# Router one chunk behind the output projection, shared experts beside the lists, and the last expert blocks in one accumulator

## The chip, the cores and the metric

The kernel runs on one core of a Trainium2 chip. The metric is device time in microseconds (us) of one execution, the median of several. The core's engines run instruction streams of their own: PE (TensorE, matrix products and transposes), DVE (VectorE), ACT (ScalarE), POOL (GpSimd) and SP (SyncE, which here only issues DMA transfers). The granted clock of PE is a number from 0 to 1 beside each stretch of a profile.

## The reference

One block of a diffusion model on 512 tokens of width 1024: a token mixer (retention and gated DeltaNet over the whole grid of tokens, merged by gates), its output projection, and a mixture of experts. The change touches what comes behind the mixer's merge. Cut to that:

```python
x  = x + g1 * _rmsnorm(merged @ w_o, norm_mix_post)          # 512 x 1024
h2 = _rmsnorm(x, norm_ffn_pre) * (1.0 + sc2) + sh2
x  = x + g2 * _rmsnorm(_moe(h2), norm_ffn_post)
...
def _moe(h):                       # 64 experts of width 256, 8 for each token
    scores = sigmoid(h @ w_router) # biased; top 4 of 8 groups, then top 8 experts
    wts = scores of the 8 chosen / their sum * 2.5
    routed[token] += wts * ((silu(xe @ w_gate[e]) * (xe @ w_up[e])) @ w_down[e])
    shared = (silu(h @ w_sh_gate) * (h @ w_sh_up)) @ w_sh_down
    return routed + shared
```

## The kernel before

The kernel is written in stages for a framework that schedules instructions: each engine keeps one program order, tiles from rotating pools make an instruction wait until the buffer's last reader is done, and semaphores are put in by the framework. The written order sets the order on each engine only roughly (a scheduler moves instructions between neighbours), so the engine orders shown under the change are those of the built programs.

**phaseO** is the output projection with all that depends on it. The projection's weights come as two column halves (c = 0, 1) of 512, and each half runs over four chunks t of 128 tokens. A projection of a chunk and half is 24 matmuls (eight k steps of three, since each operand is split in a high and a low part; L111 to L113). In the second half, each chunk goes through everything before the next starts: the square and scaling of the projection (L1086, L1087), the normalisation and residual (L1093 to L1097, which give x1 and store it to `out`), the pre-normalised row `h2` (L1099 to L1103, stored to `h2d` for the gathers), eight transposes of it (L1110) copied into `h2T` (L1111), the router `router(t)` (16 matmuls L1010, a sigmoid L1012, 26 small instructions on DVE L1013 to L1039 that give `sel` and the weights `wt`), and the shared expert `shared(t)` (64 matmuls L1054, Silu L1057, product L1058, eight wide matmuls L1063, copies L1064, store of y to the accumulator `accd[0]` in DRAM, L1065). `accd[1]` is filled with zeros (L1117).

**phaseM** starts the loads of the first experts' weights (L1156, buffers of 1 MB each: four `w`, two `wgu` that share memory with earlier tiles, three `wd`), and then makes the list of tokens for each expert: `left` is loaded (L1165) and multiplied by the transposed selection `selT` (L1167), eight rounds of maximum and replacement (L1171, L1173) sort out 64 slots for each expert and half of the tokens, and one matmul (L1178) and L1180 make `slots`. The gathers (L1190, POOL) fetch `h2` rows by these slots, the transposes L1198 turn them, and then the experts run: for each expert two projections with weights converted to high and low parts (ACT L1134, DVE L1136), Silu, a transpose, the down projection (L1229, eight matmuls), and a scatter with addition (L1234, POOL) into `accd[0]` or `accd[1]` in turn. One more block, number 64, takes the first overflow of experts with over 128 tokens, and a loop takes the rest (with this data it runs zero times). At the end the two accumulators are loaded (L1416 on SP, L1417 on ACT), added (L1418), squared (L1421), normalised (L1424) and added to `out` by an accumulating DMA (L1425, POOL).

```python
down(aT, SL[e - 1], W[e - 1], raw(e - 1, 2), (e - 1) % 2)     # last argument: accumulator
raw = lambda e, n: DW[e % 3] if n == 2 else GU[(2 * e + n) % 6]  # weight buffers
```

Of the kernel before, what the change touches and what calls it, by code (L numbers as in the profile page):

```python
# [19 lines left out]
D = 1024  # L20
# [51 lines left out]
class K:  # L72
# [903 lines left out]
    def phaseO(self):  # L976
# [72 lines left out]
        def shared(t):  # L1049
# [6 lines left out]
            sg = q.tile([128, 256], F32, name="shg")  # L1056
            nc.scalar.activation(sg, ps[:, 0:256], AF.Silu)  # L1057
            tt(sg, sg, ps[:, 256:512], op=OP.mult)  # L1058
            y = self.rawp.tile([128, 1024], F32, name="y", tag="raw")
            for c in range(2):  # L1060
                ps = self.pa()
                for k in range(2):
                    nc.tensor.matmul(ps, sg[:, k * 128:k * 128 + 128], wsh[2][:, k, c * 512:c * 512 + 512], start=k == 0, stop=k == 1)  # L1063
                nc.scalar.copy(y[:, c * 512:c * 512 + 512], ps)  # L1064
            nc.sync.dma_start(self.accd[0][ts_], y)  # L1065
# [6 lines left out]
        for c in range(2):  # L1072
            s = slice(c * 512, c * 512 + 512)
            us = [self.unit([wo[:, k0:k0 + 2, s]], 2, 512) for k0 in (0, 2, 4, 6)]
            if c:
                for w, n in zip(wsh, ("w_sh_gate", "w_sh_up", "w_sh_down")):
                    nc.sync.dma_start(w, a[n][0].rearrange("(k p) f -> p k f", p=128))
            for t in range(4):
                ps = self.pa()
                ts_ = slice(t * 128, t * 128 + 128)  # L1080
                for k in range(8):
                    h, l = us[k // 2]
                    mh, ml = self.mg[t // 2]
                    mt = slice(t % 2 * 128, t % 2 * 128 + 128)
                    self.mm3(ps, mh[:, k, mt], ml[:, k, mt], h[:, k % 2], l[:, k % 2], k == 0, k == 7)
                nc.scalar.activation(junk[:, 0:512], ps, AF.Square, accum_out=st[:, t, c:c + 1])  # L1086
                tt(mix[t][:, s], ps, rows[0][:, s], op=OP.mult)  # L1087
                if c == 0:
                    continue
                xt = q.tile([128, 1024], F32, name="xr")  # L1090
                nc.sync.dma_start(xt, a["x"][0, t * 128:t * 128 + 128])
                r = q.tile([128, 2], F32, name="rr")
                tt(r[:, 0:1], st[:, t, 0:1], st[:, t, 1:2], op=OP.add)  # L1093
                self.rsqrt(r[:, 0:1], r[:, 0:1], 1.0 / D, EPS)
                x1 = mix[t]
                stt(x1, x1, r[:, 0:1], xt, op0=OP.mult, op1=OP.add)
                nc.sync.dma_start(self.out[t * 128:t * 128 + 128], x1)  # L1097
                h2 = q.tile([128, 1024], F32, name="h2")
                tt(h2[:, 0:512], x1[:, 0:512], rows[2][:, 0:512], op=OP.mult)  # L1099
                nc.gpsimd.tensor_tensor(h2[:, 512:1024], x1[:, 512:1024], rows[2][:, 512:1024], op=OP.mult)  # L1100
                nc.scalar.activation(junk, x1, AF.Square, accum_out=r[:, 1:2])
                self.rsqrt(r[:, 1:2], r[:, 1:2], 1.0 / D, EPS)
                stt(h2, h2, r[:, 1:2], rows[1], op0=OP.mult, op1=OP.add)  # L1103
                nc.sync.dma_start(self.h2d[t * 128:t * 128 + 128, 0:1024], h2)
                self.d("h2", h2, t)
                for cc in range(2):
                    ps = self.pi()
                    for k in range(4):
                        kk = cc * 4 + k
                        nc.tensor.transpose(ps[:, k * 128:k * 128 + 128], h2[:, kk * 128:kk * 128 + 128], self.ident)  # L1110
                    nc.scalar.copy(self.h2T[:, cc * 4:cc * 4 + 4, ts_], ps.rearrange("p (k n) -> p k n", k=4))  # L1111
                router(t)
                shared(t)
# [7 lines left out]
    def phaseM(self):  # L1121
# [58 lines left out]
        ts(slots, ps[:, 0:64], -1.0, 512.0, op0=OP.mult, op1=OP.add)  # L1180
        xg6, xg3 = q.tile([128, 3, 1088], F32, name="xg", bufs=1), self.hxpool.tile([128, 3, 1088], F32, name="xg", tag="b1")
# [196 lines left out]
        for e in range(NE + 2):  # L1378
# [11 lines left out]
            if e > 0:  # L1390
                down(aT, SL[e - 1], W[e - 1], raw(e - 1, 2), (e - 1) % 2)
                load(e + 2, 2)
            make(e + 2, 1)
            prepare(e + 4)


        cnt = nc.values_load(nx[0:1, 0:1], min_val=0, max_val=62)
        with tc.For_i(0, cnt) as _:
# [10 lines left out]
            down(turn_act(act(pgu[:, 0:256], pgu[:, 256:512])), ix, ws, raw(NE, 2), 0)  # L1409


        m = self.hxpool.tile([128, 4, 1024], F32, name="fm", tag="b1")
        r = q.tile([128, 4], F32, name="fr")
        for t in range(4):
            m1 = self.rawp.tile([128, 1024], F32, name="fm1", tag="raw")
            nc.sync.dma_start(m[:, t], self.accd[0][t * 128:t * 128 + 128])  # L1416
            nc.scalar.dma_start(m1, self.accd[1][t * 128:t * 128 + 128])  # L1417
            tt(m[:, t], m[:, t], m1, op=OP.add)  # L1418
            self.d("moe", m[:, t], t)
# [28 lines left out]
```

## Time and profile before

| what | us |
|---|---|
| median of 3 runs | 1502.15 |
| the three runs | 1498.96 to 1503.06 |
| profiled execution, its own time | 1494.84 |
| its span | 1493.1 |
| PE busy in the span | 1348.6 (90%) |
| DVE, ACT, POOL busy | 903.3, 661.4, 403.9 |

The profiled execution is one of its own, not one of the three timed. Its span runs from the first to the last recorded instruction. An engine's idle time costs something only where the others wait for it, so the busy shares of the whole span say little; rows of single stretches are shown further down.

### The profile page before, as it was taken

Reading aid. Unit: us, or ns where it says so; the run is one execution under the profiler, and the core shown is the slowest. Engines: PE = TensorE matmul, PEld = TensorE weight load, DVE = VectorE, ACT = ScalarE, POOL = GpSimd, SP = SyncE. Lnnn points to the kernel's source line nnn. Section 1 sums busy time; section 2 is a strip of 40 time slices with the busy share of each in tenths; the row PEclk is TensorE's granted clock in tenths of the full one; section 3 lists DMA queues with packets and bytes.
Section 4 is the critical chain, followed back from the end, with each engine's and each line's share of the span. In section 5 each row is a group of like instructions: output and inputs, shape, how many; then the busy total and the mean of one; then the engine's idle time right before and its main releaser. Section 6 shows DMA issues by size and latency. Waiting matters only on the chain.

```text
span 1493.1 us, 20722 instructions
## 1 busy us (share of the span) xinstructions
PE 1348.6 (90%) x7848; PEld 1095.0 (73%) x7848; DVE 903.3 (60%) x1266; ACT 661.4 (44%) x931; POOL 403.9 (27%) x332
## 2 busy tenths in 40 slices
PE   6898988999999999967749999999999999999990
PEld 2667877897887777756647878878788787887770
DVE  5646795467765565432448666666666666666642
ACT  5533443544232223322315555565555555655531
POOL 0314546755120000010031222222222222223412
PEclk9999989999999999987779999999999999999995
DMA  8633412004235675721467999999999999999936
GB/s 304 182 105 93 117 43 67 15 29 124 58 100 183 210 238 164 261 98 74 156 251 262 348 353 361 353 361 351 357 359 363 363 358 362 364 357 354 327 94 177
DMA packets 138554, 339.47 MB, mean 227 GB/s; under 512 B 28187, under 2 KB 84543, under 8 KB 113493
## 3 DMA queue, kind: packets, MB, share of 16 engines
q1 hardware_dynamic: 110808, 288.94, 54.1%
q0 software_dynamic: 19872, 40.04, 10.8%
q10 hardware_dynamic: 7772, 9.14, 2.1%
q8 instruction: 63, 1.03, 0.3%
q14 instruction: 39, 0.31, 0.1%
HBM read 325.54 MB, written 48.31 MB: 250 GB/s over the span
## 4 chain that ended last, share of the span: by engine, by line
PE 43%; DMA 3%; issue 2%; DVE 1%; POOL 1%; POOLq 0%; ACT 0%; ACTq 0%; DVEq 0%
PE cs L1229 14%; PE acc L111 8%; PE acc L112 8%; PE acc L113 8%; PE ci L1198 4%; DMA wd<-in_w_down_dram 2%; PE acc L1218 1%; DMA fm<-acc 1%; PE ci L1054 1%; DVE wl L1136 0%; DMA acc<-y,sl_i 0%; DMA xg<-h2d,slots 0%; POOL xg L1184 0%; PE ci L1010 0%; DVE fm L1418 0%
## 5 line engine op out<-in xcount | busy, mean ns | idle before, releaser
L111 PE MATMUL acc<-wh,xT 128*128 128x256 f32 x1040 | 305.1, 293 | 0.1
L113 PE MATMUL acc<-wh,xT 128*128 128x256 f32 x1040 | 294.5, 283 | 0.0
L112 PE MATMUL acc<-wl,xT 128*128 128x256 f32 x1040 | 294.1, 283 | 0.0
L1136 DVE TENSOR_TENSOR wl<-w,wh 128x2048 fp32r<-128x2048 f32 x88 | 202.6, 2303 | 100.6 <-PE acc L112 94.0
L1229 PE MATMUL cs<-wd,aT 128*128 128x512 f32 x520 | 234.3, 593 | 3.4 <-DMA wd<-in_w_down_dram 2.6
L1234 POOL DMA_INDIRECT acc<-y,slots x64 | 101.6, 1587 | 478.0 <-ACT y L1231 436.0
L1134 ACT CAST wh<-w 128x2048 fp32r<-128x2048 f32 x88 | 167.3, 1901 | 97.9 <-PE acc L113 83.6
L111 PEld LDWEIGHTS acc<-wh,xT 128*128 128x128 f32 x1040 | 199.6, 192 | 0.5 <-ACT xT L1200 0.3
L112 PEld LDWEIGHTS acc<-wl,xT 128*128 128x128 f32 x1040 | 199.4, 192 | 0.2 <-issue 0.2
L113 PEld LDWEIGHTS acc<-wh,xT 128*128 128x128 f32 x1040 | 198.8, 191 | 0.0
L1229 PEld LDWEIGHTS cs<-wd,aT 128*128 128x128 f32 x520 | 93.9, 190 | 97.3 <-issue 95.1
L1201 DVE TENSOR_TENSOR xT<-ci,xT 128x512 fp32r<-128x512 f32 x130 | 89.0, 686 | 95.0 <-ACT xT L1200 94.9
L100 ACT CAST wu<-raw 128x1024 fp32r<-128x1024 f32 (+1 forms) x73 | 75.0, 1036 | 109.9 <-DMA raw<-in_w_in_dram 68.3
L1136 DVE TENSOR_TENSOR wl<-wgu,wh 128x2048 fp32r<-128x2048 f32 x42 | 96.2, 2291 | 41.6 <-PE acc L112 39.5
L111 PE MATMUL acc<-hTx,wu 128*128 128x512 f32 (+1 forms) x296 | 119.2, 403 | 1.7 <-ACT wu L100 1.7
L113 PE MATMUL acc<-hTx,wu 128*128 128x512 f32 (+1 forms) x296 | 118.1, 399 | 0.8 <-DVE wu L107 0.8
L112 PE MATMUL acc<-hLx,wu 128*128 128x512 f32 (+1 forms) x296 | 118.4, 400 | 0.0
L107 DVE TENSOR_TENSOR wu<-raw,wu 128x1024 fp32r<-128x1024 f32 (+1 forms) x61 | 77.3, 1275 | 63.7 <-ACT wu L100 63.6
L1134 ACT CAST wh<-wgu 128x2048 fp32r<-128x2048 f32 x42 | 79.7, 1898 | 50.5 <-PE acc L113 42.6
L1198 PEld LDWEIGHTS ci<-ident,xg 128*128 128x128 f32 x520 | 73.8, 192 | 34.7 <-issue 29.0
L1198 PE MATMUL ci<-ident,xg 128*128 128x128 f32 x520 | 80.5, 280 | 5.1 <-DMA xg<-h2d,slots 5.1
L1200 ACT CAST xT<-ci 128x512 fp32r<-128x512 f32 x130 | 75.8, 583 | 11.5 <-PE ci L1198 11.4
(491 smaller groups left out, 2386.3 us busy)
## 6 DMA issues: line engine op xcount, KB each, us to landing
wd<-in_w_down_dram SPq DMA_DIRECT2D x64, 1024.0 KB
w<-in_w_gate_dram SPq DMA_DIRECT2D x43, 1024.0 KB
w<-in_w_up_dram SPq DMA_DIRECT2D x43, 1024.0 KB
raw<-in_w_in_dram SPq DMA_DIRECT2D x56, 512.0 KB
wgu<-in_w_gate_dram SPq DMA_DIRECT2D x21, 1024.0 KB
wgu<-in_w_up_dram SPq DMA_DIRECT2D x21, 1024.0 KB
mraw<-in_w_mod_dram SPq DMA_DIRECT2D x32, 512.0 KB
wm<-in_w_mod_dram SPq DMA_DIRECT2D x16, 512.0 KB
```

The lines of the kernel that those rows point to most:

```text
L100: nc.scalar.copy(dst, src)
L107: (self.nc.gpsimd if eng == "pool" else self.nc.vector).tensor_tensor(dst, src, hi.bitcast(F32), op=OP.subtract)
L111: mm(out, ah, bh, start=start, stop=False)
L112: mm(out, ah, bl, start=False, stop=False)
L113: mm(out, al, bh, start=False, stop=stop)
L1134: nc.scalar.copy(h[:, i:i + max(n, 1024)], w[:, i:i + max(n, 1024)])
L1136: eng(l[:, i:i + n], w[:, i:i + n], h[:, i:i + n].bitcast(F32), op=OP.subtract)
L1198: nc.tensor.transpose(ps[:, k * 128:k * 128 + 128], xv[:, :, c * 4 + k], self.ident)
L1200: nc.scalar.copy(h, ps)
L1201: tt(l, ps, h.bitcast(F32), op=OP.subtract)
L1229: nc.tensor.matmul(ps, aT[:, m], wd[:, s], start=k == 0, stop=k == 1)
L1234: nc.gpsimd.indirect_dma_start(self.accd[acc][:, :], bass.IndirectOffsetOnAxis(ap=sx, axis=0), y[:, :], None, bounds_check=511, oob_is_err ...
```

## The change

The loop over chunks is taken apart into `proj`, `post`, `turn` (transposes and router), `shared_up` and `shared_down`. In the second half, `turn` runs one chunk behind `proj` and `post`. Only chunk 0's shared expert stays in phaseO; those of chunks 1 to 3 are written behind `slots` in phaseM. The y stores of the shared experts go from SP's to ACT's queue. In the experts, blocks 61 to 64 and the loop all add to `accd[1]`, so `accd[0]` is complete earlier, and it is loaded on SP at step 62 into weight buffers that are no longer needed, with the x1 rows of chunks 2 and 3. The tail loads only `accd[1]`, and for chunks 2 and 3 adds x1 on DVE and writes plainly.

```diff
+        def shared_up(t):
...
+            sg = sgs[t] = mp.tile([128, 256], F32, name="shg", bufs=2)
             nc.scalar.activation(sg, ps[:, 0:256], AF.Silu)
             tt(sg, sg, ps[:, 256:512], op=OP.mult)
+
+        def shared_down(t):
...
-            nc.sync.dma_start(self.accd[0][ts_], y)
+            nc.scalar.dma_start(self.accd[0][t * 128:t * 128 + 128], y)
+        self.shared = lambda t: (shared_up(t), shared_down(t))
...
+        us = weights(0)
+        for t in range(4):
+            proj(us, t, 0)
+        us = weights(1)
...
+        for t in range(4):
+            proj(us, t, 1)
+            post(t)
+            if 0 < t < 3:
+                turn(t - 1)
+        shared_up(0)
+        turn(2)
+        turn(3)
+        shared_down(0)
...
         ts(slots, ps[:, 0:64], -1.0, 512.0, op0=OP.mult, op1=OP.add)
+        for t in range(1, 4):
+            self.shared(t)
...
-                down(aT, SL[e - 1], W[e - 1], raw(e - 1, 2), (e - 1) % 2)
+                down(aT, SL[e - 1], W[e - 1], raw(e - 1, 2), 1 if e - 1 > NE - 4 else (e - 1) % 2)
...
+            if e == NE - 2:
+                halves = lambda w: [w[:, i * 1024:i * 1024 + 1024] for i in range(2)]
+                m0 = halves(raw(e, 0)) + halves(raw(e, 1))
+                x1 = halves(raw(e + 1, 0)) + halves(raw(e + 1, 1))
+                for t in range(4):
+                    nc.sync.dma_start(m0[t], self.accd[0][t * 128:t * 128 + 128])
+                for t in range(2, 4):
+                    nc.sync.dma_start(x1[t], self.out[t * 128:t * 128 + 128])
...
+        m = halves(raw(NE, 0)) + halves(raw(NE, 1))
         for t in range(4):
-            m1 = self.rawp.tile([128, 1024], F32, name="fm1", tag="raw")
-            nc.sync.dma_start(m[:, t], self.accd[0][t * 128:t * 128 + 128])
-            nc.scalar.dma_start(m1, self.accd[1][t * 128:t * 128 + 128])
-            tt(m[:, t], m[:, t], m1, op=OP.add)
+            (nc.scalar if t % 2 else nc.sync).dma_start(m[t], self.accd[1][t * 128:t * 128 + 128])
+        for t in range(4):
+            tt(m[t], m[t], m0[t], op=OP.add)
...
-            nc.gpsimd.dma_start(self.out[t * 128:t * 128 + 128], m[:, t], accum_op=OP.add)
+            if t < 2:
+                nc.gpsimd.dma_start(self.out[t * 128:t * 128 + 128], m[t], accum_op=OP.add)
+            else:
+                tt(m[t], m[t], x1[t], op=OP.add)
+                (nc.scalar if t % 2 else nc.sync).dma_start(self.out[t * 128:t * 128 + 128], m[t])
```

In the orders below a row is an operation, its result and its operands, and xN counts equal neighbours; lines of the changed kernel are 2 to 24 higher (L1087 is now L1090, L1096 L1101, L1103 L1108, L1110 to L1111 L1117 to L1118, L1054 L1056, L1063 L1067, L1134 L1156, L1136 L1158, L1178 L1200, L1198 L1222).

DVE of before, from the scaling of chunk 3's projection (L1087) to its normalised row h (L1103); `wl<-w` is the low part of an expert weight:

```order
L1087 TENSOR_TENSOR mix_4973<-acc,mrow_4934 128x512
L1093 TENSOR_TENSOR rr<-ost 128x1
L126 TENSOR_SCALAR rr<-rr 128x1
L1096 SCALAR_TENSOR_TENSOR mix_4973<-mix_4973,rr,xr 128x1024
L1099 TENSOR_TENSOR h_5580<-mix_4973,mrow_4936 128x512
L1136 TENSOR_TENSOR wl<-w,wh 128x2048
L126 TENSOR_SCALAR rr<-rr 128x1
L1103 SCALAR_TENSOR_TENSOR h_5580<-h_5580,rr,mrow_4938 128x1024
```

DVE of the change, from the conversion ahead of the same scaling (now L1090) to the residual of that chunk (L1101); L1017 to L1024 belong to the router of chunk 1:

```order
L1158 TENSOR_TENSOR wl<-w,wh 128x2048
L1038 TENSOR_SCALAR wt<-wt,sm_4966 128x64
L1017 TENSOR_TENSOR sm_4966<-t_4963 128x8
L1090 TENSOR_TENSOR mix_4973<-acc,mrow_4934 128x512
L1020 TENSOR_TENSOR rA<-sm_4966 128x64
L1021 TENSOR_TENSOR rB<-sm_4966 128x64
L1098 TENSOR_TENSOR rr<-ost 128x1
L1158 TENSOR_TENSOR wl<-w,wh 128x2048
L1023 TENSOR_TENSOR rB<-rB,c_glt 128x64
L126 TENSOR_SCALAR rr<-rr 128x1
L1024 TENSOR_TENSOR rA<-rA,rB 128x64
L1101 SCALAR_TENSOR_TENSOR mix_4973<-mix_4973,rr,xr 128x1024
```

The row of chunk 3 had one conversion between its steps; now it has one between them, one ahead of them, and router instructions in between.

ACT of before, from the square of chunk 3's projection (L1086) to its router's sigmoid (L1012):

```order
L1086 ACTIVATE ojunk,ost<-acc 128x512
L1134 CAST wh<-w 128x2048
L1101 ACTIVATE ojunk,rr<-mix_4973 128x1024
L1134 CAST wh<-w 128x2048
L1111 COPY h2T<-ci 128x4x128 x2
L1012 ACT_TABLE_LOAD
L1012 ACTIVATE scr<-ci 128x64
```

ACT of the change, from the same square (now L1089) to the sigmoids of chunks 2 and on; L1118 copies transposes into `h2T`:

```order
L1089 ACTIVATE ojunk,ost<-acc 128x512
L1156 CAST wh<-w 128x2048 x2
L1106 ACTIVATE ojunk,rr<-mix_4973 128x1024
L1059 ACT_TABLE_LOAD
L1059 ACTIVATE shg<-ci 128x256
L1118 COPY h2T<-ci 128x4x128 x2
L1012 ACT_TABLE_LOAD
L1012 ACTIVATE scr<-ci 128x64
L1118 COPY h2T<-ci 128x4x128 x2
```

The copies of chunk 2's transposes (the first L1118) now stand behind chunk 3's square, two casts, its second square and the Silu of shared expert 0.

PE of before, from the last chunk's transposes to the transposes of gathered tokens (L1198):

```order
L1110 MATMUL ci<-ident,h_5580 128x128 x8
L1010 MATMUL ci<-wr,h2T 128x64 x8
L1054 MATMUL ci<-h2T,wsh 128x128 x23
L1043 MATMUL cs<-ident,sel 128x128
L1054 MATMUL ci<-h2T,wsh 128x128 x9
L1063 MATMUL acc<-wshd,shg 128x512 x4
L1178 MATMUL ci<-c_i_4950,left 128x64
L1198 MATMUL ci<-ident,xg 128x128 x16
```

PE of the change, from the first half of shared expert 0's down projection to the transposes of gathered tokens (now L1222):

```order
L1067 MATMUL acc<-wshd,shg 128x512 x2
L1010 MATMUL ci<-wr,h2T 128x64 x8
L1067 MATMUL acc<-wshd,shg 128x512 x2
L1043 MATMUL cs<-ident,sel 128x128
L1200 MATMUL ci<-c_i_4950,left 128x64
L1056 MATMUL ci<-h2T,wsh 128x128 x43
L1067 MATMUL acc<-wshd,shg 128x512 x4
L1056 MATMUL ci<-h2T,wsh 128x128 x26
L1067 MATMUL acc<-wshd,shg 128x512 x4
L1056 MATMUL ci<-h2T,wsh 128x128 x27
L1222 MATMUL ci<-ident,xg 128x128 x8
L1067 MATMUL acc<-wshd,shg 128x512 x4
```

Three shared experts have moved from ahead of the list's matmul (now L1200) to behind it, and the transposes of gathered tokens stand among the last of them.

## Rows read from the trace of the kernel before

**Rows 1.** The page's slices of the span, 40 equal ones, tenths of full speed.

```profile
PEclk9999989999999999987779999999999999999995
```

**Rows 2.** Busy time by window: span, engines, granted clock, DMA share, GB/s.

```profile
633.00:781.00 148.00, 92.71 (x486) 78.71 (x486) 55.40 (x179) 37.47 (x56) 24.17 (x26) 0.77 0.38 144
...
860.00:1400.00 540.00, 540.00 (x3443) 438.70 (x3442) 360.15 (x315) 312.01 (x365) 142.59 (x105) 1.00 1.00 358
```

**Rows 3.** The chain that ended last, 633 to 785: start, length, what.

```profile
772.46 3.93 DMA xg<-h2d,slots
...
780.45 0.37 PE acc L111
```

**Rows 4.** Groups by form, 633 to 781: count, busy, mean ns, idle before.

```profile
L1136 DVE TENSOR_TENSOR wl<-w,wh 128x2048 fp32r<-128x2048 f32 x3 | 7.9, 2646 | 15.6 <-PE acc L112 9.0 <-PE acc L113 6.5
L1110 PE MATMUL ci<-ident,h 128*128 128x128 f32 x32 | 7.8, 425 | 33.8 <-DVE h L1103 33.8
...
L1012 ACT ACT_TABLE_LOAD x4 | 5.1, 1283 | 0.1
...
L1178 PE MATMUL ci<-c_i,left 128*128 128x64 f32 x2 | 0.7, 435 | 12.7 <-ACT left L1175 12.7
```

**Rows 5.** PE in order of time, 632.5 to 685: start, length, instruction.

```profile
632.74 0.39 PE L113 MATMUL acc<-wu,ml 128*128 128x512 f32 x1
640.67 1.97 PE L1110 MATMUL ci<-ident,h 128*128 128x128 f32 x8 [7.54 <-DVE h L1103]
642.46 3.68 PE L1010 MATMUL ci<-wr,h2T 128*128 128x64 f32 x16
...
659.14 0.39 PE L112 MATMUL acc<-wu,mh 128*128 128x512 f32 x1
...
664.16 0.39 PE L113 MATMUL acc<-wu,ml 128*128 128x512 f32 x1
```

**Rows 6.** The chain that ended last, 1380 to 1494.

```profile
1390.03 30.18 DMA wd<-in_w_down_dram
...
1420.35 3.67 PE cs L1229 x8
1424.02 0.44 PE ci L1198 x4
...
1459.59 4.56 DMA acc<-y,sl_i
1465.25 4.61 DMA fm<-acc
...
1477.67 1.23 DVE fm L1418
```

**Rows 7.** DVE in order of time, 728 to 784.

```profile
745.07 0.23 DVE L1013 TENSOR_TENSOR cand<-scr,rbias 128x64 f32<-128x64 f32 x1 [5.88 <-ACT scr L1012]
...
749.73 0.25 DVE L1038 TENSOR_SCALAR wt<-wt,sm 128x64 f32<-128x64 f32 x1
...
762.33 0.42 DVE L1167 TENSOR_TENSOR left<-cs,left 128x256 f32<-128x256 f32 x1 [6.89 <-DMA left<-in_cst_dram]
...
770.20 0.19 DVE L1176 COPY left<-left 64x64 f32<-64x64 f32 x1
771.35 0.22 DVE L1180 TENSOR_SCALAR slots<-ci 128x64 int32<-128x64 f32 x1 [0.96 <-PE ci L1178]
```

**Rows 8.** SP's queue, 830 to 1400: what its issues waited for.

```profile
SPq L1156 <- DVE wl L1136: 284.4, 55, 5.3
...
SPq L1156 <- DMA w<-in_w_up_dram: 0.4, 1, 0.4
```

**Rows 9.** SP's queue in order of time, 700 to 850.

```profile
753.42 0.33 SPq L1156 DMA_DIRECT2D wgu<-in_w_gate_dram  x1
```

**Rows 10.** POOL in order of time, 1444 to 1494.

```profile
1454.85 1.55 POOL L1234 DMA_INDIRECT acc<-y,slots  x1 [7.87 <-ACT aT L1220]
...
1483.91 0.86 POOL L1425 DMA_DIRECT2D out_dram<-fm  x1 [0.79 <-DVE fm L1424]
```

More of the change, by code (lines that the diff above doesn't have):

```diff
@@ L1047, in phaseO @@
         wsh = [b1[:, 0], b1[:, 1], k0_]
-        def shared(t):
+        sgs = {}
+        def shared_up(t):
             ts_ = slice(t * 128, t * 128 + 128)
@@ L1055, in shared @@
                                      start=k == 0, stop=k == 7)
-            sg = q.tile([128, 256], F32, name="shg")
+            sg = sgs[t] = mp.tile([128, 256], F32, name="shg", bufs=2)
             nc.scalar.activation(sg, ps[:, 0:256], AF.Silu)
             tt(sg, sg, ps[:, 256:512], op=OP.mult)
+        def shared_down(t):
             y = self.rawp.tile([128, 1024], F32, name="y", tag="raw")
@@ L1062, in shared @@
                 for k in range(2):
-                    nc.tensor.matmul(ps, sg[:, k * 128:k * 128 + 128], wsh[2][:, k, c * 512:c * 512 + 512], start=k == 0, stop=k == 1)
+                    nc.tensor.matmul(ps, sgs[t][:, k * 128:k * 128 + 128], wsh[2][:, k, c * 512:c * 512 + 512], start=k == 0, stop=k == 1)
                 nc.scalar.copy(y[:, c * 512:c * 512 + 512], ps)
-            nc.sync.dma_start(self.accd[0][ts_], y)
+            nc.scalar.dma_start(self.accd[0][t * 128:t * 128 + 128], y)
+        self.shared = lambda t: (shared_up(t), shared_down(t))
         wo = a["w_o"][0].rearrange("(k p) n -> p k n", p=128)
@@ L1071, in phaseO, with weights, proj @@
         junk = p.tile([128, 1024], BF, name="ojunk")
-        for c in range(2):
+        def weights(c):
+            return [self.unit([wo[:, k0:k0 + 2, c * 512:c * 512 + 512]], 2, 512) for k0 in (0, 2, 4, 6)]
+        def proj(us, t, c):
             s = slice(c * 512, c * 512 + 512)
[L1074 to L1113, printed above, removed]
@@ new lines, in proj, with post @@
+            ps = self.pa()
+            mh, ml = self.mg[t // 2]
+            mt = slice(t % 2 * 128, t % 2 * 128 + 128)
+            for k in range(8):
+                h, l = us[k // 2]
+                self.mm3(ps, mh[:, k, mt], ml[:, k, mt], h[:, k % 2], l[:, k % 2], k == 0, k == 7)
+            nc.scalar.activation(junk[:, 0:512], ps, AF.Square, accum_out=st[:, t, c:c + 1])
+            tt(mix[t][:, s], ps, rows[0][:, s], op=OP.mult)
+        h2s = {}
+        def post(t):
+            xt = q.tile([128, 1024], F32, name="xr")
+            nc.sync.dma_start(xt, a["x"][0, t * 128:t * 128 + 128])
+            r = q.tile([128, 2], F32, name="rr")
+            tt(r[:, 0:1], st[:, t, 0:1], st[:, t, 1:2], op=OP.add)
+            self.rsqrt(r[:, 0:1], r[:, 0:1], 1.0 / D, EPS)
+            x1 = mix[t]
+            stt(x1, x1, r[:, 0:1], xt, op0=OP.mult, op1=OP.add)
+            nc.sync.dma_start(self.out[t * 128:t * 128 + 128], x1)
+            h2 = h2s[t] = q.tile([128, 1024], F32, name="h2")
+            tt(h2[:, 0:512], x1[:, 0:512], rows[2][:, 0:512], op=OP.mult)
+            nc.gpsimd.tensor_tensor(h2[:, 512:1024], x1[:, 512:1024], rows[2][:, 512:1024], op=OP.mult)
+            nc.scalar.activation(junk, x1, AF.Square, accum_out=r[:, 1:2])
+            self.rsqrt(r[:, 1:2], r[:, 1:2], 1.0 / D, EPS)
+            stt(h2, h2, r[:, 1:2], rows[1], op0=OP.mult, op1=OP.add)
+            nc.sync.dma_start(self.h2d[t * 128:t * 128 + 128, 0:1024], h2)
+            self.d("h2", h2, t)
@@ new lines, in turn @@
+        def turn(t):
+            for cc in range(2):
+                ps = self.pi()
+                for k in range(4):
+                    kk = cc * 4 + k
+                    nc.tensor.transpose(ps[:, k * 128:k * 128 + 128], h2s[t][:, kk * 128:kk * 128 + 128], self.ident)
+                nc.scalar.copy(self.h2T[:, cc * 4:cc * 4 + 4, t * 128:t * 128 + 128], ps.rearrange("p (k n) -> p k n", k=4))
+            router(t)
+        us = weights(0)
+        for t in range(4):
+            proj(us, t, 0)
@@ L1114, in phaseO @@
+        us = weights(1)
+        for w, n in zip(wsh, ("w_sh_gate", "w_sh_up", "w_sh_down")):
+            nc.sync.dma_start(w, a[n][0].rearrange("(k p) f -> p k f", p=128))
+        for t in range(4):
[7 more added lines that the diff above has]
+        shared_down(0)
         z = self.rawp.tile([128, 1024], F32, name="zero", tag="raw")
```

9 lines of the change are left out of this document (4 added, 5 removed).

## The prediction

> **What bounds the kernel now.** I read the page's slices first, then busy time by stage, then the chain and the groups of the slow stage, then single instructions in order of time. In the slices [rows 1] the reader is to see one soft place: three near the middle where the clock granted to TensorE (PE) falls to 0.7. The windows [rows 2] give it borders. From 633, where chunk 0's projection of the second half ends, to 781, where the first expert starts, PE works 92.71 of 148 us, at a mean clock of 0.77. From 860 to 1400, in the experts, PE works all 540 us at 1.00. So 55 us of PE idle time, and the low clock behind it, lie in the part that the change rearranges; what is saved ahead of the first expert matmul (780.45, [rows 3]) moves every expert forward, as long as their weights keep up.
>
> The groups [rows 4] say what most of the 55 us are: 33.8 us ahead of the transposes L1110, which wait for the normalised row h, and 12.7 ahead of L1178, which waits for the slot list. The gather takes 3.93 us more [rows 3]. Chunk 0 is the pattern [rows 5]: its projection ends at 632.74 + 0.39 = 633.13, the transposes start 7.54 us later. Those 8 then take 1.97 us and the 16 router matmuls 3.68; in the experts 4 transposes take 0.44 [rows 6], 0.11 each against 0.24. [...]
>
> **The front part, step by step.** Units at full clock: a projection is 24 matmuls at 0.228 us (22 steps from 659.14 to 664.16, [rows 5]) = 5.5; a turn is 8 transposes (0.9) and 16 router matmuls (half of 3.68 = 1.8); a shared expert is 64 matmuls, by the transposes' 0.11 each 7.1, and 8 wide ones, 3.67 by L1229's equal ones [rows 6], = 10.8.
>
> *To the last projection.* From 633.1: three projections (16.5), two turns (5.4), and waits of some 3 us, since h of chunk 0 is ready 7.54 us after its projection and the next projection covers 5.5 of that. Projection 3 ends at 658; with the turns still at half clock at 663.
>
> *Its normalised row.* The order of DVE in the change shows what is new: between the scaling of projection 3 (L1090) and its row (L1101, later L1108) stand a weight conversion and router instructions of chunk 1, with another conversion just ahead. The bare chain is 7.5, a conversion 2.65 on average [rows 4], a router 749.98 − 745.07 = 4.9 [rows 7]: 7.5 + 2 × 2.65 + 4.9 = 17.7. With part of the first conversion under the projection I take 17: the row at 675. Meanwhile PE has shared_up(0) (658 to 665) and the transposes of chunk 2, whose copies stand on ACT behind two casts, a square and a table load (the order of ACT). PE so idles some 7 us between 666 and 675, and works at half clock again.
>
> *Last router, list.* From 675: transposes 2.0, their copy some 0.6, the router's 3.7, with shared_down(0) between (3.7): scores at 685. Most of the router's 4.9 on DVE, 4.0, leads to the selection: 689.7 with the score's activation. The list: 762.33 to 770.39 = 8.1 [rows 7]; with some 2 us of other DVE work interposed, a transpose and the slots it ends at 701.5, where it ended at 771.57. The load for its first operand, for which DVE waited 6.89 us [rows 7], issues on ACT behind the copy of shared_down(0) at about 683, and is in by 690: hidden. PE idles some 10 us.
>
> *What is put behind the list.* Three shared experts, 3 × 10.8 = 32.4, and 16 transposes of gathered tokens, 1.8; the gather (3.93) is hidden under the first shared expert. The half clock costs about 4.6 us of the first 10. Sum 38.8: first expert matmul at **740.3** instead of 780.45, **−40**. Checked by kind: PE's idle time falls from 55 to about 21 (3 + 7 + 10, and 1), −34, and the low clock is worth −6.
>
> Bounds: full clock in the shared experts (−4.6) and chunk 3's row after 14 us instead of 17 give −48; half clock through two shared experts (+5) and projection 3 at 662 give −31. That ACT loads its tables less often (the router's and Silu's functions switch less) and that the y store issues on ACT instead of SP I cost at nothing: ACT is busy 37.47 of 148 us [rows 2]. Without that cover a table load is 1.28 [rows 4], an issue 0.33 by SP's [rows 9].
>
> [...]
>
> **The experts** move as a block if their weights do. SP's issues in 830 to 1400 wait for DVE's conversions 284.4 us in all and for a transfer 0.4 [rows 8]: for consumers, and an earlier consumer frees its buffer earlier. New is that the gate and up weights of expert 2 share a buffer with the shared experts' weights, and so issue only after shared_up(3), at about 735 instead of 753.42 [rows 9], with SP's later loads behind them. That is 5 us ahead of the first expert instead of 27. Two loads of 1 MB at the stage's 358 GB/s [rows 2] are 5.9 us: they land at 741 to 743 and are wanted at about 744, behind two experts' conversions. I cost 0, bound 3.
>
> Against that speaks the DMA share of 1.00 in 860 to 1400 [rows 2]. But PE waits for nothing there, with 540.00 of 540 us. [...]
>
> **The tail.** The last scatters (expert 63 and the extra one) now hit one accumulator. They were issued at 1454.85 and 1459.59 [rows 10], the last landing after 4.56 [rows 6]. If the second must wait for the first's landing, 1454.85 + 4.6 = 1459.45: 0; the bound is 1.5, another issue behind. Loads: four of 0.5 MB instead of eight, of which the first pair landed 4.61 us after 1465.25 and the last let DVE start at 1477.67 [rows 6]. With half of them all could be in by 1472, but then DVE is the bound: six adds and four scalings of 1024 columns, at the 1.23 of the last add [rows 6] 12.3 us, from the first landing at 1469.9, so with waits for the squares between them the last write issues at 1482 to 1483.4, against 1483.91 [rows 10]. It is a plain write where it was an accumulating one. I take −2, with bounds +1.5 and −6 (loads and plain write both give all they can).
>
> The sum: −40 − 2 = −42, from the profiled 1494.84 to 1453. The runs' median stands 7.3 above the profiled execution, so **1460**, written 1461 for the loads at the start.
>
> **Rivals.** *The loads take it back* (10%). A down-projection load issued at 1390.03 landed after 30.18 us [rows 6], so near the end transfers lag; were the stage bound by them, a start 40 earlier with loads only 18 earlier would return about half: 1480. For it: share 1.00. Against: PE without idle time. *Clock or queues are worse* (15%): −31 − 1: 1470. *They are better* (15%): −48 − 3: 1451. *The tail does nothing* (inside the forecast's range): 1463, the wait for loads handed to DVE. *Slower* (3%): SP's one queue stands at the wait for shared_up(3), and while it stands no later weights are loaded. From experts 2 to 4 getting their weights 42 us late in all, the time of 14 loads at 358 GB/s, the change is slower: with 50 us about 1510.
>
> [...]
>
> **How the numbers follow.** The forecast, with −36 to −46, has 50%; better 15%, worse 15%, the loads 10%, something between them and no change 7%, slower 3%. The range, 1447 to 1477, takes the first three. 0.3% (4.5 us) is about what a measurement can tell here. Faster by over that: 0.94; within: 0.03; slower: 0.03.
>
> **What would show it.** Right: the first expert matmul at 735 to 749; about 21 us of PE idle time ahead of it, some 10 of them before the list's matmul; three shared experts between list and experts in some 39 us; no PE idle time in the experts; the end of the span about 41 us earlier. Wrong: idle PE in the second to fourth expert with a load as releaser; half clock through all shared experts; the second scatter over 2 us behind the first one's landing.

## The result and the profile after

The change takes 1449.37 us (median of 4 runs, 1448.30 to 1450.15) where the kernel before takes 1502.25 (four runs, one more than in the table above): ratio 0.965, 95% interval 0.9635 to 0.967, 52.9 us less. I had forecast 1461 with a range of 1447 to 1477. The direction and the place were right; the gain was taken 11.6 us too small. The time is near the lower end of the range and is that of the rival "they are better" (15%, 1451), not of the forecast's own stretch of −36 to −46.

The profiled execution of the change has a span of 1448.4 us (time 1450.15). First the page's clock by slices, then windows (columns as in [rows 2]): the front stretch from the square of chunk 0's second projection to the first expert matmul, in the kernel before (633.23 to 780.26) and in the change, and a stretch of the change's experts:

```profile
PEclk9899999999999999999899999999999999999995
```

```profile
633.23:780.26 147.03, 91.84 (x483) 77.97 (x483) 54.84 (x178) 36.98 (x56) 24.17 (x26) 0.77 0.38 144
...
637.05:736.42 99.37, 78.71 (x482) 65.93 (x481) 51.60 (x177) 30.83 (x51) 23.49 (x25) 0.90 0.52 189
...
860.00:1330.00 470.00, 470.00 (x3005) 382.63 (x3004) 311.99 (x276) 272.13 (x319) 121.52 (x91) 1.00 1.00 359
```

The soft place of [rows 1] has shrunk to one slice at 0.8. The front stretch is 99.4 us instead of 147.0, PE is busy in 78.7 of it instead of 91.8, and its mean clock is 0.90 instead of 0.77. The reader can split the gain with this one pair of rows: idle time 55.2 to 20.7, −34.5, and busy time −13.1 for the same matmuls (483 and 482 records), which goes with the higher clock. In the experts PE has no idle time from 860 to 1330, and one pause of 2.07 us later (shown further down).

PE in order of time, the instructions behind a wait and those that tell the clock:

```profile
644.52 1.09 PE L1117 MATMUL ci<-ident,h 128*128 128x128 f32 x8 [1.68 <-DVE h L1108]
...
654.49 1.06 PE L1117 MATMUL ci<-ident,h 128*128 128x128 f32 x8 [0.69 <-DVE rB L1023]
...
674.04 0.33 PE L1043 MATMUL cs<-ident,sel 128*128 128x128 f32 x1 [4.28 <-DVE sel L1034]
674.21 1.52 PE L1010 MATMUL ci<-wr,h2T 128*128 128x64 f32 x8
677.38 0.48 PE L1117 MATMUL ci<-ident,h 128*128 128x128 f32 x1 [1.65 <-DVE shg L1060]
...
679.25 1.70 PE L1117 MATMUL ci<-ident,h 128*128 128x128 f32 x7
...
682.80 1.90 PE L1010 MATMUL ci<-wr,h2T 128*128 128x64 f32 x16
...
690.37 0.33 PE L1043 MATMUL cs<-ident,sel 128*128 128x128 f32 x1 [3.90 <-DVE sel L1034]
699.11 0.66 PE L1200 MATMUL ci<-c_i,left 128*128 128x64 f32 x2 [8.41 <-ACT left L1197]
699.56 12.56 PE L1056 MATMUL ci<-h2T,wsh 128*128 128x128 f32 x86
...
736.42 0.36 PE L111 MATMUL acc<-wh,xT 128*128 128x256 f32 x1
```

The transposes of chunks 0 and 1 wait 1.68 and 0.69 us (the first waited 7.54 before, [rows 5]) and take 1.09 and 1.06 us, at a granted clock of 1.00 in the waits and in the transposes. What the prediction calls half clock is 0.50 in the trace of before: in the wait of 7.54 us the clock is 1.00 up to 638, and it is 0.50 from 639 on and in the 8 transposes and 16 router matmuls behind the wait. In the change it is still 1.00 in the wait of 4.28 and falls right behind it, to 0.50 from 675 on: the 8 router matmuls there take 1.52, 0.19 each, and after the next wait of 1.65, 7 of chunk 3's transposes take 1.70, 0.24 each, at 0.50. It has risen by the last router (16 matmuls in 1.90, 0.12 each, at 1.00). It is 1.00 in the wait of 3.90 us too, falls in the one of 8.41 (0.50 from 691.7 on) and stays at 0.50 up to 705: 86 matmuls take 12.56, 0.146 each, against 0.11. The waits of 1.68 and 0.69 us between full work left the clock up here; run e5, below, has one of 2.13 us with slower matmuls behind it. By groups (as in [rows 4]):

```profile
L1056 PE MATMUL ci<-h2T,wsh 128*128 128x128 f32 x256 | 32.0, 290 | 0.0
...
L1010 PE MATMUL ci<-wr,h2T 128*128 128x64 f32 x64 | 9.1, 301 | 0.0
...
L1117 PE MATMUL ci<-ident,h 128*128 128x128 f32 x32 | 5.4, 314 | 4.0 <-DVE h L1108 1.7 <-DVE shg L1060 1.7 <-DVE rB L1023 0.7
```

The routers cost 9.1 us of PE for the same 64 matmuls (14.7 by the same view of before, 425 ns each on the mean instead of 301), the transposes 5.4 against 7.8 [rows 4].

For the comparison of all runs I cut each profiled execution in three: front, from the square of chunk 0's second projection on ACT (633.23 before, 637.05 in the change) to the first expert matmul; experts, to the start of the last down projection; tail, to the end of the span. "Below" is the median against that of the kernel before in the same session.

| kernel | below, us | front | experts | tail |
|---|---|---|---|---|
| before | | 147.0 | 674.6 | 38.2 |
| the change | 52.9 | 99.4 | 676.6 | 35.4 |
| e1 front alone | 47.6 | 99.0 | 675.3 | 40.7 |
| e2 tail alone | 5.6 | 147.8 | 671.5 | 34.5 |
| e3 front, one accumulator, no preload | 46.3 | 98.8 | 677.5 | 40.5 |
| e4 change, all writes accumulating | 46.4 | 99.1 | 677.0 | 40.0 |
| e5 lag, shared experts before the list | 46.5 | 108.9 | 675.2 | 34.4 |
| e6 shared experts moved, no written lag | 43.3 | 108.5 | 677.8 | 35.1 |
| e7 shared experts in one piece before the list | 45.9 | 105.6 | 675.2 | 34.5 |
| e8 one shared expert ahead of the list | 60.3 | 90.6 | 675.6 | 36.2 |
| e9 before, one ring changed | 34.7 | 108.9 | 676.1 | 38.7 |
| e10 before again | −0.9 | 148.7 | 676.9 | 38.7 |
| e11 the change again | 54.4 | 99.4 | 674.4 | 36.0 |
| e12 e8 with a tail of plain writes | 64.8 | 89.8 | 675.3 | 33.5 |

### The profile page after: what moved, and what is told of

Its sections match the earlier page's. It is cut to its first block, busy times and chain, and to the rows that moved or that the text cites. A ratio compares the mean times of both kernels' runs of the same rounds, so it can differ in the third digit from the quotient of the medians.

```text
span 1448.4 us, 20720 instructions
## 1 busy us (share of the span) xinstructions
PE 1338.8 (92%) x7848; PEld 1085.2 (75%) x7848; DVE 901.3 (62%) x1268; ACT 655.7 (45%) x927; POOL 404.1 (28%) x330
## 4 chain that ended last, share of the span: by engine, by line
PE 66%; DVE 8%; DMA 8%; POOL 2%; issue 2%; ACT 1%; SPq 0%; ACTq 0%; DVEq 0%; POOLq 0%
PE cs L1253 15%; PE acc L113 12%; PE acc L112 12%; PE acc L111 12%; PE ci L1222 4%; DMA raw<-in_w_in_dram 2%; PE ci L1056 2%; DMA wd<-in_w_down_dram 2%; DVE wu L107 1%; PE acc L1242 1%; PE acc L1067 1%; DMA mraw<-in_w_mod_dram 1%; ACT wu L100 1%; PE ci L596 1%; PE cs L655 1%
## 5 line engine op out<-in xcount | busy, mean ns | idle before, releaser
L1158 DVE TENSOR_TENSOR wl<-w,wh 128x2048 fp32r<-128x2048 f32 x88 | 201.6, 2291 | 87.4 <-PE acc L112 86.0
L1156 ACT CAST wh<-w 128x2048 fp32r<-128x2048 f32 x88 | 167.3, 1901 | 100.7 <-PE acc L113 85.6
L1158 DVE TENSOR_TENSOR wl<-wgu,wh 128x2048 fp32r<-128x2048 f32 x42 | 96.3, 2292 | 41.5 <-PE acc L112 41.4
L1156 ACT CAST wh<-wgu 128x2048 fp32r<-128x2048 f32 x42 | 79.7, 1898 | 50.0 <-PE acc L113 42.1
L1222 PEld LDWEIGHTS ci<-ident,xg 128*128 128x128 f32 x520 | 73.4, 192 | 29.8 <-issue 29.5
L1214 POOL DMA_INDIRECT xg<-h2d,slots x64 | 71.3, 1113 | 31.6 <-issue 18.0
L1222 PE MATMUL ci<-ident,xg 128*128 128x128 f32 x520 | 80.0, 278 | 0.0
```

The costliest lines, as they stand in the source:

```text
L1156: nc.scalar.copy(h[:, i:i + max(n, 1024)], w[:, i:i + max(n, 1024)])
L1158: eng(l[:, i:i + n], w[:, i:i + n], h[:, i:i + n].bitcast(F32), op=OP.subtract)
L1214: nc.gpsimd.indirect_dma_start(xg[:, :], None, self.h2d[:, :], bass.IndirectOffsetOnAxis(ap=ix, axis=0), bounds_check=511, oob_is_err=False)
L1222: nc.tensor.transpose(ps[:, k * 128:k * 128 + 128], xv[:, :, c * 4 + k], self.ident)
```

## Experiments

**Which part gives what (e1, e2).** Each part alone: e1 has the tail of before, e2 the front of before.

> The order of the change in phaseO and phaseM with the tail of before (accumulators in turn, eight loads, four accumulating writes). Theory A (nearly all of the gain comes from the stretch ahead of the first expert; the tail is worth some 3 us, as 34.5 to 31.7 us between the last down projection and the end of the span say): 46 to 52 us below before, 2 to 5 us above the change. Theory B (the tail's share is larger, and what the two traces do not explain, 52.9 us by the medians against 44.7 by the spans, lies there): 40 to 46 us below before, 7 to 12 above the change.

> The kernel before with the tail of the change alone (blocks 61 to 64 in one accumulator, the other preloaded, plain write of two chunks). Theory A: 2 to 4 us below before. Theory B: 7 to 12 us below. My forecast had taken 2.

Measured 1452.87 (47.6 below 1500.5) and 1494.88 (5.6 below; ratio 0.9952 to 0.9977). The two add up to 53.2, the change has 52.9. By the traces theory A holds for the front (147.0 to 99.0); the tail, at 5.6, is worth more than A's 2 to 4 and less than B's 7. The old tail does not take the same time everywhere: 38.2 and 38.7 us behind the old front, 40.7 behind the new one (e1), with the same instructions; no run shows why. So by the traces the new tail is worth 2.8 us against the kernel before (3.7 in e2) and 5.3 against e1; the medians say 5.6 for e2, and 5.3 for the change against e1.

**The tail's pieces (e3, e4).** e3 adds to e1 only the choice of the accumulator; e4 is the change without the plain write:

```diff
 e3, against e1
-  down(..., (e - 1) % 2)
+  down(..., 1 if e - 1 > NE - 4 else (e - 1) % 2)
 e4, against the change
-  if t < 2:
+  if t < 4:
       nc.gpsimd.dma_start(self.out[...], m[t], accum_op=OP.add)
```

> The front of the change, blocks 61 to 64 in one accumulator, but nothing preloaded: eight loads and four accumulating writes as before. It is the price of the one accumulator by itself. If the extra block's scatter waits for the landing of expert 63's, it issues some 1 us after its data is ready (1418.48 against 1417.4 in the change), and the time is 0.5 to 1.5 us above the run with the front alone. If neighbours collide in more places: 4 us or more above.

> The change with all four chunks written by accumulating DMA, no addition of x1 on DVE. If the plain write pays (from its issue to the end of the span 5.5 us in the change, 9.2 us from the last accumulating one before), the time is 1.5 to 3 us above the change; if DVE's two additions cost as much as the shorter landing gives, it is equal within 1 us.

e3: 1454.25, 1.4 above e1, intervals that overlap; its tail by the trace is not longer than e1's (40.5 and 40.7). The scatters on POOL show a small cost; the second one:

```profile
1417.98 1.55 POOL L1258 DMA_INDIRECT acc<-y,sl_i  x1 [3.88 <-DMA acc<-y,slots]
```

It waits for the first one's landing and issues 5.4 us after the last down projection starts, against 4.7 before: 0.7 us. e4: 1454.09 in its session, 46.4 below before, where the change has 52.9 and 54.4; that is 6.5 to 8 us above the change, more than either branch of the expectation. By the traces its tail is 40.0 us where those with a plain write have 33.5 to 36.2. So with accumulating writes the preload and the single accumulator give 0.7 us at most (e1 40.7, e3 40.5, e4 40.0), and the plain write of two chunks 4.6 (40.0 to 35.4): nearly the whole gain of the tail. POOL of e4, the last three of the four writes:

```profile
1434.25 3.84 POOL L1458 DMA_DIRECT2D out_dram<-w  x3
```

The last of these issues before 1438.1, and the span ends at 1448.3. In the change the last plain write issues on ACT's queue at 1442.94 and the span ends at 1448.4:

```profile
1442.94 0.34 ACTq L1461 DMA_DIRECT2D out_dram<-w  x1
```

**What in the front counts (e5, e6, e7, e9).** e5 keeps the lag and puts the shared experts back between the chunks; e6 drops the written lag and keeps them behind the list; e7 puts three in one piece before the list; e9 is the kernel before with one word changed.

```diff
 e5, against the change (and no shared experts in phaseM)
+            if t:
+                turn(t - 1)
+                self.shared(t - 1)
+        turn(3)
+        self.shared(3)
 e6, against the change
             post(t)
-            if 0 < t < 3:
-                turn(t - 1)
+            turn(t)
         shared_up(0)
-        turn(2)
-        turn(3)
 e7, against the change (and no shared experts in phaseM)
         shared_down(0)
+        for t in range(1, 4):
+            self.shared(t)
 e9, against before, in shared(t)
-                ps = self.pa()
+                ps = self.pc()
```

> The change with all four shared experts in phaseO, each behind the turn of its chunk, one chunk behind the projection; nothing stands beside the list. Theory P (the lag does most: the 33.8 us of waits for h go, and what the shared experts cover behind the list is only the gather and the wait for the list's operand): first expert matmul 3 to 10 us later than in the change, time 3 to 10 us above it. Theory Q (covering the list is half of the gain, since 12.7 + 5.1 us of idle time stood there and the low clock behind them): 18 to 25 us above the change.

> The change with each turn written straight behind its chunk's normalisation, and the shared experts of chunks 1 to 3 behind the list; shared expert 0 behind the last router. In the built program PE's order still has the projection of chunk 1 ahead of the transposes of chunk 0, since no shared expert of a chunk stands any more between two projections. Theory P, in the form that it is the projections' freedom to run ahead that counts and not the written lag: within 6 us of the change, above or below. If the written lag counts: the idle time ahead of the transposes comes back in part, 15 to 30 us above the change.

> The change with the shared experts of chunks 1 to 3 between the last router and the list, in one piece, instead of behind the list. DVE's list then starts behind the last shared expert's product: 8.1 us of rounds and 4 to 5 us of gather with nothing on PE. Against it the 8.4 us that PE stood before the list in the change are gone. Sum 3 to 6 us above the change, with 2 to 3 of that from the low clock at the first expert. If the place of the shared experts does not matter: within 1 us.

> The kernel before with one word changed: the shared expert's down projection takes its accumulators from the ring cs instead of the ring acc, which the projections use. In the built program the projection of chunk 1 then stands ahead of the transposes of chunk 0, and so on, with nothing else of the change. Theory P (it is the projections' freedom to run ahead that gives most of the gain; the run with the lag alone was 46.5 us below before with the tail's 5 in it): 33 to 42 us below before. Theory W (the written lag and the split of the shared expert are needed): less than 20 us below before.

Measured: e5 1454.76, 46.5 below before, so 6.4 less than the change's 52.9; e6 1457.99, 43.3; e7 1455.39, 45.9; e9 1466.22, 34.7 below before with nothing of the change in it. P holds for e5 and e9: with either half alone, and with the ring alone, 38 us of the front's 48 are there (108.9, 108.5 and 108.9 us). e6 misses both of its branches: it is 9.6 us above the change, more than P's 6 and less than the 15 to 30 for the case that the written lag counts. Beside the moved shared experts the lag is worth some 9 us of the front (108.5 to 99.4). e7, 7.0 above, is just over its 3 to 6 (front 6.2 longer): the place of the shared experts counts. In e9 the front is 108.9 us and PE busy in 80 of it at a clock of 0.87:

```profile
637.00:746.00 109.00, 80.08 (x479) 66.26 (x478) 54.12 (x178) 36.43 (x55) 24.07 (x26) 0.87 0.52 194
```

Only the accumulator ring of the shared expert's down projection differs there. With it, the scheduler by itself puts the next chunk's projection ahead of the waiting transposes, and these wait 1.68 us where it was 7.54 [rows 5]; with the shared ring it did not. Of its transposes (L1110) those of chunk 1 do not wait at all; the others in order of time:

```profile
644.89 1.09 PE L1110 MATMUL ci<-ident,h 128*128 128x128 f32 x8 [1.68 <-DVE h L1103]
...
680.91 1.06 PE L1110 MATMUL ci<-ident,h 128*128 128x128 f32 x8 [1.62 <-DVE h L1103]
...
704.97 1.94 PE L1110 MATMUL ci<-ident,h 128*128 128x128 f32 x8 [6.57 <-DVE h L1103]
```

Why the scheduler goes by the ring is not shown by any run.

PE of e5, its first transposes, the second half of that chunk's router, and the shared expert's matmuls behind it:

```profile
640.80 1.09 PE L1117 MATMUL ci<-ident,h 128*128 128x128 f32 x8 [2.13 <-DVE h L1108]
...
643.58 1.81 PE L1010 MATMUL ci<-wr,h2T 128*128 128x64 f32 x8
645.18 9.40 PE L1056 MATMUL ci<-h2T,wsh 128*128 128x128 f32 x62
```

The wait is 2.13 us, hardly more than the 1.68 of the change, but what follows is a router in small pieces, with 0.24 us of waiting for a copy ahead of it, and not a projection. The 8 router matmuls take 0.23 us each and the 62 of the shared expert 0.15. In the change 8 of a router take 1.81 us, 0.23 each, at a granted clock of 0.50, and 64 of a shared expert 7.30, 0.11 each, at 1.00; from these times I estimate that the clock fell in e5. Whether it was the router or the longer wait no run shows.

The waits that are left in e5 around the list and the gather:

```profile
733.21 0.66 PE L1199 MATMUL ci<-c_i,left 128*128 128x64 f32 x2 [14.41 <-ACT left L1196]
738.54 3.67 PE L1219 MATMUL ci<-ident,xg 128*128 128x128 f32 x16 [4.67 <-DMA xg<-h2d,slots]
```

14.41 and 4.67 us: what the shared experts cover in the change is the gather and part of the list. In e6 the transposes (L1117) of the later chunks still wait, and the list (L1197) too:

```profile
665.81 1.94 PE L1117 MATMUL ci<-ident,h 128*128 128x128 f32 x8 [4.42 <-DVE sm L1026]
...
679.80 1.94 PE L1117 MATMUL ci<-ident,h 128*128 128x128 f32 x8 [6.78 <-DVE cand L1031]
...
708.85 0.66 PE L1197 MATMUL ci<-c_i,left 128*128 128x64 f32 x2 [9.58 <-ACT left L1194]
```

e7's PE has both waits in one place, behind all of its shared work, 12.54 and 4.70:

```profile
735.68 0.66 PE L1202 MATMUL ci<-c_i,left 128*128 128x64 f32 x2 [12.54 <-ACT left L1199]
741.04 3.65 PE L1222 MATMUL ci<-ident,xg 128*128 128x128 f32 x16 [4.70 <-DMA xg<-h2d,slots]
```

**Filling what is left (e8, e12).** e8 splits one shared expert around the list's matmul:

```diff
+        self.shared1 = shared_up(1)      # ends in phaseO; returns the product's call
 ...
         ts(slots, ...)
+        self.shared1()                   # the product on DVE
+        self.shared_down(1)
+        for t in range(2, 4):
+            self.shared(t)
```

> The change with one shared expert's first matmuls (chunk 1) ahead of the list's matmul and its product on DVE behind the list's rounds. If the 8.4 us in which PE stands before the list's matmul in the change are its real remaining cost, they are filled with 7 us of work: first expert matmul 7 to 10 us earlier, time 6 to 10 us below the change. If the product on DVE delays the list, or the experts' weights (issued behind the last shared expert) cannot follow, 0 to 3 us below.

Measured 1440.98, 60.3 below before, ratio 0.957 to 0.963; the change has 0.9635 to 0.967, and 0.9626 to 0.968 when run again (e11). The front is 8.8 us shorter than the change's, as expected. PE around the list:

```profile
691.05 0.33 PE L1043 MATMUL cs<-ident,sel 128*128 128x128 f32 x1 [1.01 <-DVE sel L1034]
...
698.62 2.50 PE L1067 MATMUL acc<-wshd,shg 128*128 128x512 f32 x4 [2.99 <-DVE shg L1060]
700.91 0.53 PE L1202 MATMUL ci<-c_i,left 128*128 128x64 f32 x2
```

The waits of 3.90 and 8.41 have become 1.01 and 2.99, and the front is 90.6 us. The loads that issue behind the last shared expert kept up (experts 675.6). e12 adds to e8 a tail without accumulating writes, with x1 of all four chunks loaded ahead:

```diff
+            tt(m0[t], m[t], g2p, op=OP.mult)          # before r is known
 ...
+            nc.vector.scalar_tensor_tensor(m[t], m0[t], r[:, t:t + 1], x1[t], op0=OP.mult, op1=OP.add)
+            (nc.scalar if t % 2 else nc.sync).dma_start(self.out[...], m[t])
```

> The kernel with one shared expert ahead of the list, and a tail without accumulating writes: x1 of all four chunks preloaded, the gain multiplied in before the row's scale is known, so that one DVE pass (scale, plus x1) and a plain write follow it. In the trace of the change the accumulating writes move some 200 GB/s with the DMA engines at 0.9 busy, the plain ones 400 and more. Theory C (the accumulating writes' drain sets the end of the tail): from the last down projection to the end of the span 33 to 35 us instead of 36.1, 1 to 3 us below the kernel with one shared expert ahead. Theory D (DVE's chain sets the end; it has 12 passes of 1.23 us in place of 10): 36.5 to 38.5 us, up to 2 us above.

Measured 1435.93 (64.8 below before, ratio 0.955 to 0.958). The tail is 33.5 us although DVE has two passes more; by the traces that is 2.7 below e8, as expected, and by the medians the whole kernel is 4.5 below, more than the 1 to 3. DVE's last four passes run without a gap from 1424.25:

```profile
1424.25 4.86 DVE L1461 SCALAR_TENSOR_TENSOR w<-wgu,fr,w 128x1024 f32<-128x1024 f32 x4
```

Theory C. The last pass ends 29.5 us after the start of the last down projection, so the last write is hardly earlier than the change's (30.0); what is shorter is what follows it, 4.0 us instead of 5.4. This is the fastest version.

**Scatter (e10, e11).** The same two kernels once more.

> The kernel before once more, for a second profiled execution. Its first one took 1494.84 us, 7.4 us less than the median of its timed runs, and I carried those 7.3 us over to the change. If they are a scatter of single executions: a profiled execution between 1494 and 1506 with the stretch from chunk 0's square to the first expert at 147 us within 1 us, and the difference elsewhere. If the kernel's front stretch itself varies: 147 to 155 us there.

> The change once more, beside the two others, for a second profiled execution: front stretch 99.4 us within 1 us, experts 676 to 678, tail 35 to 36, and 50 to 54 us below before. If the first measurement of 52.9 was a lucky pair of medians: 45 to 49 below.

e10: median 1501.87, its profiled execution 1498.88; front 148.7 (1.7 over the first one, at a clock of 0.75), experts 2.2 and tail 0.5 longer. So the front of the kernel before is not the same within 1 us, and its gain is 47.6 to 49.3. e11: 1446.53, 54.4 below; front 99.4 again, experts 674.4, below the 676 to 678 that I expected. Single executions differ by more in other places: the start of the front alone lies between 632.2 and 639.2 in the fourteen executions of the table.

## Why the prediction was right, and where its sizes were off

**The front, −40 forecast, −47.6 measured.** The chain came out nearly as worked. ACT's square of chunk 3's projection and its copies of chunk 2's transposes, chunk 3's row on DVE, the sigmoid of the last router and the slots, in the change:

```profile
661.84 0.60 ACT L1089 ACTIVATE ojunk<-acc 128x512 bf16<-128x512 f32 x1 [2.76 <-PE acc L113]
...
673.51 1.07 ACT L1118 COPY h2T<-ci 128x512 f32<-128x512 f32 x2
...
675.71 1.29 DVE L1108 SCALAR_TENSOR_TENSOR h<-h,rr,mrow 128x1024 f32<-128x1024 f32 x1 [0.66 <-POOL rr L127]
...
684.73 0.22 ACT L1012 ACTIVATE scr<-ci 128x64 f32<-128x64 f32 x1 [1.15 <-DMA left<-in_cst_dram]
...
699.80 0.22 DVE L1202 TENSOR_SCALAR slots<-ci 128x64 int32<-128x64 f32 x1 [0.95 <-PE ci L1200]
```

Projection 3 ends 24.8 us after the start (24.9 forecast, 658 − 633.1); chunk 3's row is ready 15.2 us after it instead of 17. PE's pause meanwhile, some 7 forecast, is 4.28 + 1.65. I had put it on the copies of chunk 2's transposes; the row names the selection of chunk 1 on DVE as what ended it at 674.04, and the copies end at 674.58, so both held PE about equally long.

The first expert matmul comes 99.4 us after the start instead of 107.2 (740.3 − 633.1). Of the 7.8 us, 1.9 are there when the row is ready, 2.3 lie between it and the last router's score, 1.2 in the selection and the list (slots 63.0 instead of 68.4 after the start), and 2.4 in the shared experts with the 16 transposes (36.4 instead of 38.8). The term that was mis-sized is "the low clock is worth −6": it is −13.1. I had let the last routers, the transposes and shared_down(0) run at the low level (0.50) up to 685, but the last router took 1.90 us at a granted clock of 1.00, not 3.7; and behind the list I had charged 4.6 us, where 86 matmuls in 12.56 are 3.1 more than at 0.11 each. The slower bound's half clock through two shared experts did not come in the change: 0.50 ended at 705, within the first one behind the list.

My check by kind hid this. By the prediction's own times PE has almost nothing to do between the score at 685 and the list's matmul just before 701.5, so its pause there comes to some 15 us and not 10, the idle time to 26 and not 21, and the low clock to −11 and not −6. Measured are 12.3 us (3.90 + 8.41) and 20.7 in all. That the idle time met the 21 is partly luck. Of my bounds the time is at the faster one (−48), but what I gave as its reasons, full clock in the shared experts and an earlier row, is only some 3.4 of the 7.8 us (1.5 and 1.9).

**The experts, 0.** Right in the sum: 676.6 against 674.6, with 671.5 to 677.8 over the runs. The first of the late weights, the gate weights of expert 2, issue at 730.97 (some 735 forecast), and PE waits for no weights near the start: from 736 to 860 its one wait is 3.2 us, for `colx` from DVE. The rival that the loads take the gain back falls: e12 starts the experts 57 us earlier than before and keeps 675.3. One of my signs, "no PE idle time in the experts", was not met: a load of `wd` that landed after 29.44 us, as late as the one in [rows 6], cost 2.07 us near the end.

```profile
1366.65 5.37 PE L1253 MATMUL cs<-wd,aT 128*128 128x512 f32 x8 [2.07 <-DMA wd<-in_w_down_dram]
```

**The tail, −2.** By the trace it gave −2.8, but not in the way that I worked out, so the near hit is luck. I had the last write issue 0.5 to 2 us earlier; it issues 1.0 later (30.0 us after the start of the last down projection, against 29.0 before, [rows 10]). The gain lies behind it: from the last issue to the end of the span 5.4 us instead of 9.2. The step "then DVE is the bound" failed: DVE sets when the last write can issue (its last addition ends at 1442.90, the write issues at 1442.94), but the accumulating writes to `out`, which move some 200 GB/s, set the end. DMA activity in 40 slices over 18 us (kernel before, from 1476), and over 11.4 us (the change, from 1437):

```profile
DMA  9709900599892959999999999999989000000000
GB/s 419 291 9 55 91 0 0 109 182 246 173 264 46 146 100 146 228 209 191 219 173 218 191 228 191 228 191 209 200 173 246 9 0 0 0 0 0 0 0 0
```

```profile
DMA  0000994988999996989999999899999998000000
GB/s 0 0 0 0 101 129 43 129 115 172 230 230 230 201 201 101 201 158 230 201 201 216 230 230 216 316 402 446 417 446 417 374 431 331 14 0 0 0 0 0
```

Each digit of the first row is the DMA engines' busy share in tenths, the second row is GB/s. Before, with four accumulating writes, the rate is some 200 GB/s at a share of mostly 0.9 for some 10 us (23 slices of 0.45); in the change it does so for two writes, then some 400 GB/s for the two plain ones. e12's row, all plain, over 13 us from 1420:

```profile
DMA  0000000000000000000499999999999999950000
GB/s 0 0 0 0 0 0 0 0 0 0 0 0 0 0 0 0 0 0 0 176 403 403 416 391 403 416 391 403 403 416 403 391 416 416 403 202 0 0 0 0
```

The accumulating writes go out on POOL's queue and the plain ones on SP's and ACT's, so the queue could be the reason. The queues' lines of the change's window (packets, MB, share of the 16 engines' time in 11.4 us; q0 is POOL's), and that of POOL's queue in the kernel before, 861.6 to 863.8, where it carries a gather, which does not accumulate:

```profile
q0 software_dynamic: 288, 1.05, 53.5%
q1 hardware_dynamic: 144, 0.52, 11.4%
q10 hardware_dynamic: 144, 0.52, 11.2%
...
q0 software_dynamic: 70, 0.12, 14.6%
```

In time of all 16 engines the accumulating writes take 0.535 × 11.4 / 1.05 = 5.8 us for each MB, the plain ones 2.5, and the gather on POOL's own queue 0.146 × 2.2 / 0.12 = 2.7. So a transfer on POOL's queue is not slow for that alone, and I take the accumulation to be the reason; it is not shown, since a gather reads from DRAM, and a plain write on POOL's queue is in no run.

The one accumulator costs 0.8 us, inside 0 to 1.5. The second scatter waits 3.99 us, up to the landing of the first:

```profile
1412.93 1.56 POOL L1258 DMA_INDIRECT acc<-y,slots  x1 [5.58 <-ACT aT L1244]
1418.48 1.56 POOL L1258 DMA_INDIRECT acc<-y,sl_i  x1 [3.99 <-DMA acc<-y,slots]
```

```profile
1412.93 4.73 DMA acc<-y,slots
...
1424.30 7.97 DMA w<-acc
```

The first scatter lands 4.73 after 1412.93, the second issues at 1418.48. Half the loads did not halve their time: the last lands 7.97 us after 1424.30, where before DVE started on the last 12.4 us after ACT's first issue (1465.25 to 1477.67, [rows 6]). I had all of them in by 17 us after the start of the last down projection (1472); the last came 19.3 after it. Without the plain write this tail would have been hardly a gain (e4).

**From profile to median.** "The runs' median stands 7.3 above the profiled execution" I carried over to the change. That did not hold: its median is 0.8 below its profiled execution, and in e10 the difference is 3.0. It is scatter of single executions. It and the front's term erred in the same direction, and so the time came out near the end of the range. This offset (7.3 + 0.8) makes 8.1 of the 11.6 us. Between the profiled executions themselves I was 2.9 off (1453 to 1450.15): 7.6 in the front and 0.8 in the tail, less a start 3.8 later in this execution and experts 2.0 longer. The rest is the rounding to 1461.

## What to carry to other kernels

Where PE waits in front of small work, count what its low clock costs behind each wait beside the wait itself: here it was 13.1 of 47.6 us. In the change, waits of 0.69 and 1.68 us between projections cost none of it, at a granted clock of 1.00; behind one of 2.13 us ahead of a router, in e5, that router's second half took 0.23 us a matmul, where the change's last router took 0.12 at 1.00. A wait is best filled with work that is independent on every engine, split if need be: one shared expert's matmuls ahead of the list's and its product behind gave 6 to 7 us more than the change (60.3 below before, against 52.9 and 54.4). Before code is reordered by hand, look at what keeps the scheduler from doing it: one accumulator ring gave 34.7 us with one word, of the 52.9 that the whole change gave.

## What the runs showed of the hardware that was not expected

In these traces the accumulating DMA writes to `out` move about half of what the plain ones do, some 200 against 400 GB/s, with the DMA engines' busy share at mostly 0.9 in both. In the change they take 5.8 us of all 16 engines' time for each MB, the plain ones 2.5. It is the end of the kernel that pays: from the last issue to the end of the span 9.2 us before, 5.4 in the change with two such writes, and 4.0 in e12 with none.
